# Attention run as one sequence of rounds in a fixed TensorE order, with the softmax factors moved behind the products and some small transfers moved to GpSimd's queue

## Chip, cores and metric

The kernel runs on one core of one Trainium2 chip. The metric is the device time of one execution in microseconds, and the median of three runs is compared. A core has five engines that each work through their own list of instructions in order: TensorE (PE; its weight loads are the separate rows PEld), VectorE (DVE), ScalarE (ACT), GpSimd (POOL) and SyncE (SP, which here only issues transfers).

## The reference

One decoder layer over 1024 positions of width 1024, in float32. One projection feeds three groups of heads, whose outputs are joined, projected and added to the input; a gated feed-forward part follows.

```
h = rms_norm(x, norm_mix);  proj = h @ w_in
y_conv = conv_mixer(p_conv)          # 256 channels, causal convolution of width 31
y_nsa  = nsa_mixer(p_nsa)            # 8 query heads, 2 KV heads, head size 64
y_rwkv = rwkv7_mixer(p_rwkv)         # 4 heads x 64, a recurrence over positions
x = x + concat(y_conv, y_nsa, y_rwkv) @ w_out
h = rms_norm(x, norm_ffn);  x = x + (silu(conv3(h @ w_gate)) * (h @ w_up)) @ w_down
return rms_norm(x, norm_final)

# nsa_mixer, for each block of 128 queries:
return gate0 * o_cmp + gate1 * o_sel + gate2 * o_win
# o_cmp: attention over 63 compressed blocks; o_sel: over the selected blocks, which with
# 16 blocks of 64 keys and top 16 are all keys up to the query; o_win: over the last 512 keys
```

Each of the three is a softmax of its own: exp(scores - max), divided by its sum, times the values.

## The kernel before

The work runs in stages. Input projection, convolution and the first half of RWKV fill the span up to some 400 us. Stage "2" is attention together with the second half of RWKV. Stage "o" is the output projection; then come the two feed-forward products.

Attention goes over eight tiles of 128 queries in the order 7, 6, 5, 4, 0, 3, 2, 1 (`attn_tile`, one call for each). A tile i has two branches: the window branch (br 2, min(i+1, 5) key tiles of 128) and the selected branch (br 1, i+1 key tiles). A branch has four units (r), each for one query head of both KV heads (g). For a unit TensorE forms the scores in PSUM banks "mm" (L893 with the high part of the keys, L894 with the low part), VectorE adds the mask and finds the extreme (L897), ScalarE takes the exponential and sums it (L904), VectorE forms gate over sum (L905, L906) and scales the 128 x W probabilities with it (L911), TensorE transposes them, two key tiles at a time, into a "tr" bank (L918), ScalarE copies that bank to SBUF (L921, tile "pT"), and TensorE multiplies with the values into the tile's one bank "av" (L926), which collects both branches and the compressed one (L862 to L865). At its end the bank is copied (L932, tile "mix") and stored to `md` in DRAM. In all there are 264 pairs of unit and key tile: 528 transposes and 528 products, which the trace counts as 1056 records.

The instructions of one engine stand in an order that a scheduler picked when the kernel was built; nothing by hand holds TensorE's order in attention. RWKV's steps are emitted with high priority and fall in among the attention.

RWKV works in four units: 00 and 01 before attention, 10 and 11 during it. A unit starts (S) with products on TensorE (L493) that give GA, whose blocks go through DRAM (`dn`, L503, and L506 back into sN). A forward substitution of 31 steps follows on GpSimd (L528 and L530, each step needing the one before). Its result goes through DRAM again (`dt` L534, `dtt` L535, then DF L543 and sN L546, L547), and TensorE takes it up at L550 (step V). Then the chain of states runs (step C, L591 to L611), and its end (L631, L636) gives the gated output, stored to `md` (L638). The 19 transfers of a unit are issued by SP.

GpSimd also forms the sums of the feed-forward weights during attention (`down_sums`, L945 to L948: 44 operations of 128 x 512, their loads at L943), between the steps of unit 10's substitution, and small parts of the compressed branch (L849, L857).

Stage "o" (`out_tile`) loads the joined outputs of 128 positions from `md` (L984, tile "mix"; the first half of it holds convolution and RWKV, the second attention), splits them in two parts (L120, L121) and multiplies with w_out (L229, "woh", "wol"), in 48 products for one tile of positions. The parts of w_out are loaded at L964 and L967.

## Time and profile before

| | us |
|---|---|
| median of 3 runs (lowest, highest) | 1515.36 (1514.93, 1518.39) |
| the profiled execution | 1516.71 |
| its span | 1515.0 |
| TensorE busy in the span | 1418.2 |
| VectorE, ScalarE, GpSimd busy | 1001.0, 684.0, 500.2 |
| attention, from the first scores to the last product (start) | about 402 to 731 |

The span is what the trace covers; 1.71 us of the profiled execution lie outside it. Busy time is the sum over an engine's instructions. A granted clock of 1.00 is TensorE's full speed in that stretch.

### The profile page before, as it was taken

The page shows a single profiled execution, that of the slowest core. Times are in us where ns is not written, and L with a number is a line of the kernel's source. Part 1 is how long each engine was busy: PE and PEld are TensorE (multiplying, and loading weights), DVE is VectorE, ACT ScalarE, POOL GpSimd, SP SyncE. Part 2 cuts the span into 40 slices and gives each one's busy share as a digit, 9 for nine tenths or more (in the row PEclk, how much of TensorE's full clock was granted, in tenths as well). Part 3 has the DMA queues.
Part 4 walks back from the last instruction along what each step waited for, and adds up shares of the span by engine and source line. Part 5 has one row for each costly group of instructions (what it writes and reads, how often), then busy time and mean ns, then how long its engine had stood idle before and what let it go on. Part 6 is the DMA issues. An engine that isn't in the chain of part 4 may idle for free.

```text
span 1515.0 us, 22973 instructions
## 1 busy us (share of the span) xinstructions
PE 1418.2 (94%) x8025; PEld 1128.7 (75%) x8025; DVE 1001.0 (66%) x2171; ACT 684.0 (45%) x1361; POOL 500.2 (33%) x607
## 2 busy tenths in 40 slices
PE   6999688999798999999599899999999999999997
PEld 5887566777666777767478677888888788888886
DVE  5346696454488587777446776775876876666675
ACT  5432255534155665776333353333333443445463
POOL 1003887910487204100000133453453443113310
PEclk9999887999699999999899999999999999999999
DMA  6133223434888301310742113332332333986633
GB/s 184 36 105 80 46 77 95 146 89 119 246 259 270 101 21 41 81 43 16 226 121 84 57 56 98 105 112 84 104 119 91 104 104 111 383 295 213 207 91 111
DMA packets 206680, 186.71 MB, mean 123 GB/s; under 512 B 56355, under 2 KB 145764, under 8 KB 206564
## 3 DMA queue, kind: packets, MB, share of 16 engines
q1 hardware_dynamic: 206564, 185.24, 39.5%
q8 instruction: 63, 1.03, 0.3%
q14 instruction: 53, 0.43, 0.1%
HBM read 126.99 MB, written 58.20 MB: 122 GB/s over the span
## 4 chain that ended last, share of the span: by engine, by line
PE 78%; DVE 10%; DMA 4%; POOL 2%; issue 2%; ACT 2%; SPq 1%; DVEq 0%; ACTq 0%; POOLq 0%
PE mm L229 13%; PE gb L229 12%; PE rw L229 10%; PE ga L229 8%; PE gc L229 8%; PE tr L229 5%; PE tr L918 4%; PE av L926 4%; PE mm L893 2%; PE mm L894 2%; POOL sx L528 1%; PE rw L493 1%; POOL sT L530 1%; DVE pp L897 1%; DVE pp L911 1%
## 5 line engine op out<-in xcount | busy, mean ns | idle before, releaser
L229 PE MATMUL mm<-hT,whi 128*128 128x512 f32 x608 | 201.6, 413 | 0.0
L229 PE MATMUL mm<-hT,wlo 128*128 128x512 f32 x304 | 126.1, 416 | 18.8 <-DVE wlo L121 18.8
L229 PEld LDWEIGHTS mm<-hT,whi 128*128 128x128 f32 x608 | 118.3, 197 | 28.5 <-issue 1.4
L921 ACT ACTIVATE pT<-tr 128x512 f32<-128x512 f32 (+1 forms) x152 | 79.8, 536 | 62.1 <-PE tr L918 59.0
L926 PE MATMUL av<-pT,V 128*64 128x128 f32 x1056 | 96.4, 289 | 1.3 <-ACT pT L921 1.1
L279 POOL TENSOR_TENSOR cacc<-cacc,ctap 128x512 f32<-128x512 f32 x60 | 91.6, 1550 | 15.0 <-ACT ctap L278 14.9
L229 PE MATMUL rw<-woh,mix 128*128 128x512 f32 x240 | 79.4, 406 | 17.0 <-ACT mix L120 17.0
L918 PE MATMUL tr<-idn,pp 128*128 128x128 f32 x528 | 91.6, 292 | 0.5 <-DVE pp L911 0.3
L121 DVE TENSOR_TENSOR sp<-rb,sp 128x512 fp32r<-128x512 f32 x66 | 57.1, 865 | 50.4 <-ACT sp L120 50.3
L1072 POOL TENSOR_TENSOR S<-wraw,wr 128x512 f32<-128x512 f32 x22 | 28.5, 1295 | 181.0 <-DVE or L107 79.2
L229 PEld LDWEIGHTS mm<-hT,wlo 128*128 128x128 f32 x304 | 59.9, 197 | 37.0 <-DVE wlo L121 20.1
L893 PE MATMUL mm<-KH,QS 128*128 128x512 f32 (+2 forms) x192 | 77.3, 407 | 10.0 <-DVE mx L897 7.7
L229 PE MATMUL rw<-sp,sp 128*128 128x512 f32 x330 | 86.1, 389 | 0.0
L229 PE MATMUL tr<-sp,sp 128*128 128x512 f32 x330 | 85.9, 389 | 0.0
L926 PEld LDWEIGHTS av<-pT,V 128*64 128x64 f32 x1056 | 59.9, 138 | 27.3 <-issue 13.0
L528 POOL TENSOR_TENSOR sx<-sN,sT 128x60 f32<-128x60 f32 (+24 forms) x124 | 47.4, 382 | 97.4 <-DMA sN<-dn 90.5
L918 PEld LDWEIGHTS tr<-idn,pp 128*128 128x128 f32 x528 | 56.5, 142 | 30.0 <-issue 27.9
L120 ACT ACTIVATE sp<-rb 128x512 fp32r<-128x512 f32 x66 | 41.6, 630 | 74.0 <-PE tr L229 37.5
L121 DVE TENSOR_TENSOR sp<-b,sp 128x512 fp32r<-128x512 f32 x88 | 68.8, 789 | 5.3 <-ACT sp L120 5.1
L229 PEld LDWEIGHTS rw<-sp,sp 128*128 128x128 f32 x330 | 62.0, 188 | 12.8
L229 PEld LDWEIGHTS tr<-sp,sp 128*128 128x128 f32 x330 | 62.0, 188 | 12.8
L904 ACT ACTIVATE pp<-pp,nm 128x640 f32<-128x640 f32 (+3 forms) x64 | 57.6, 904 | 23.7 <-DVE nm L902 22.1
(457 smaller groups left out, 3721.0 us busy)
## 6 DMA issues: line engine op xcount, KB each, us to landing
wraw<-in_ffn_w_up_dram SPq DMA_DIRECT2D x44, 256.0 KB
wr<-in_ffn_w_gate_dram SPq DMA_DIRECT2D x44, 256.0 KB
pdS<-prod SPq DMA_DIRECT2D x44, 256.0 KB
b<-pdS SPq DMA_DIRECT2D x44, 256.0 KB
rb<-tdT SPq DMA_DIRECT2D x44, 256.0 KB
pdA<-prod SPq DMA_DIRECT2D x33, 256.0 KB
b<-pdA SPq DMA_DIRECT2D x33, 256.0 KB
wraw<-in_w_in_dram SPq DMA_DIRECT2D x30, 256.0 KB
```

What stands on the lines that cost most here:

```text
L120: self.nc.scalar.activation(hi, src, AF.Copy)
L121: getattr(self.nc, eng).tensor_tensor(lo, src, hi.bitcast(F32), op=ALU.subtract)
L229: mm = lambda l, r, **k: self.nc.tensor.matmul(out, l, r, skip_group_check=more, **k)
L279: nc.gpsimd.tensor_tensor(t[:, o:o + 512], t[:, o:o + 512], z, op=ALU.add)
L528: v_.tensor_tensor(x, N[:, q, q + 1:32].unsqueeze(2).to_broadcast([P, n, w]), Tm[:, q, 0:w].unsqueeze(1).to_broadcast([P, n, w]), op=ALU.mult)
L893: pe.matmul(pts[g][:, 0:n], QS[:, r, g, :], KH[g][hf][:, ks], start=True, stop=False)
L894: pe.matmul(pts[g][:, 0:n], QS[:, r, g, :], KL[g][hf][:, ks], start=False, stop=True)
L904: s.activation(Ps[g], Ps[g], AF.Exp, bias=nm[:, g:g + 1], scale=-1.0, accum_out=sm[:, g:g + 1])
L918: pe.transpose(pt[:, o:o + P], Ps[g][:, kt * P:kt * P + P], self.idn)
L921: s.activation(pT[:, 0:n], pt[:, 0:n], AF.Copy)
L926: pe.matmul(av[g * 64:g * 64 + 64, r * P:r * P + P], self.V[kk // 2][:, kk % 2, vo + g * 64:vo + g * 64 + 64], pT[:, o:o + P], start=first ...
L1072: gp.tensor_tensor(t, x, y, op=op)
```

## The change

Attention becomes one function over all tiles. It lists the units, cuts each branch into rounds, and emits round after round: the transposes of round k, then the products of round k-1, then scores for the rounds ahead, as far as the six "pp" buffers go. A round has two items; an item is two pairs of unit and key tile (which may belong to different units, so that every "tr" bank is filled with four transposes), or the four transposes of the compressed branch or of the factors. Each TensorE instruction of attention is tied behind the one emitted before it (`pe`), so their order is held; instructions of RWKV and of stage "o" may still fall in between.

The probabilities are no longer scaled. Each branch collects its products in a bank of its own turn; gate over sum is formed once for a tile and branch ([128, 8], L905 and L906 before), spread by GpSimd to a [128, 512] tile "fx", transposed by TensorE, copied by ScalarE ("fs"), multiplied with the finished bank by VectorE and added to "mix" by GpSimd. The compressed branch has a bank of its own and starts "mix".

The 19 transfers of each RWKV unit (dn, sN, dt, dtt, DF, sN) are issued by GpSimd instead of SP. In the table of numbers pT goes from 5 to 9 buffers, pk from 1280 to 1024, and a new dvc=4 gives each fourth copy of a "tr" bank to VectorE. `down_sums` is emitted at the end of each tile, as before.

```diff
-                        nc.sync.dma_start(dn[p0:p0 + 8].rearrange("p s t -> s p t"), Gm[64 + blk * 32:96 + blk * 32, :, blk * 32:blk * 32 + 32])
+                        nc.gpsimd.dma_start(dn[p0:p0 + 8].rearrange("p s t -> s p t"), Gm[64 + blk * 32:96 + blk * 32, :, blk * 32:blk * 32 + 32])
         N = self.sN.rearrange("p (a b) -> p a b", b=32)
         for g in range(4):
-            nc.sync.dma_start(N[g * 32:g * 32 + 32], dn)
+            nc.gpsimd.dma_start(N[g * 32:g * 32 + 32], dn)
...
-            nc.sync.dma_start(u.dt[:, :, g, :], Tm[g * 32:g * 32 + 16])
-            nc.sync.dma_start(u.dtt[:, :, g, :], sTT[g * 32:g * 32 + 32])
+            nc.gpsimd.dma_start(u.dt[:, :, g, :], Tm[g * 32:g * 32 + 16])
+            nc.gpsimd.dma_start(u.dtt[:, :, g, :], sTT[g * 32:g * 32 + 32])
...
-        nc.sync.dma_start(DF[64:96], u.dt.rearrange("p s g c -> s p (g c)"))
+        nc.gpsimd.dma_start(DF[64:96], u.dt.rearrange("p s g c -> s p (g c)"))
         nc.gpsimd.memset(TT[96:128, :, 0:32], 0.0)
         dtt = u.dtt.rearrange("p c g t -> (c g) p t")
-        nc.sync.dma_start(TT[64:96, :, 0:32], dtt[:, 0:16])
-        nc.sync.dma_start(TT[96:128, :, 32:64], dtt[:, 16:32])
+        nc.gpsimd.dma_start(TT[64:96, :, 0:32], dtt[:, 0:16])
+        nc.gpsimd.dma_start(TT[96:128, :, 32:64], dtt[:, 16:32])
...
-                v.reciprocal(sm, sm)
-                v.tensor_tensor(sm, sm, gt[:, r:8:4, br], op=ALU.mult)
-                for g in range(2):
-                    if g < self.B["sc"]:
-                        s.activation(Ps[g], Ps[g], AF.Copy, scale=sm[:, g:g + 1])
-                    else:
-                        v.tensor_scalar(Ps[g], Ps[g], sm[:, g:g + 1], None, op0=ALU.mult)
...
+    def pe(self, *a, transpose=False, **k):
+        ins = (self.nc.tensor.transpose if transpose else self.nc.tensor.matmul)(*a, **k)
+        if self.pe_last is not None:
+            self.tc.add_manual_dep(ins.ins, self.pe_last.name, mybir.DependencyInfo(mybir.DependencyClass.NoSync, mybir.DependencyReason.DATA),
+                                   reason="attention")
+        self.pe_last = ins.ins
+        return ins
...
+    def attn_T(self, x, units):
+        pt = self.bank("tr")
+        y = [(units[n], kt, g) for n, kt in x for g in range(2)]
+        for n, (u, kt, g) in enumerate(y):
+            self.pe(pt[:, n * P:n * P + P], u.Ps[g][:, kt * P:kt * P + P], self.idn, transpose=True)
+        pT = self.xt([P, 512], "pT")
+        self.ncopy += 1
+        if self.B["dvc"] and self.ncopy % self.B["dvc"] == 0:
+            self.nc.vector.tensor_copy(pT, pt)
+        else:
+            self.nc.scalar.activation(pT, pt, AF.Copy)
+        return [(*z, pT[:, n * P:n * P + P]) for n, z in enumerate(y)]
+    def attn_factors(self, t, br):
+        nc = self.nc
+        F = t.sums[br]
+        nc.vector.reciprocal(F, F)
+        f2 = F.rearrange("p (r g) -> p g r", g=2)
+        nc.vector.tensor_tensor(f2, f2, t.gt[:, :, br].rearrange("p (g r) -> p g r", g=2), op=ALU.mult)
+        X = self.xt([P, 512], "pT", name="fx")
+        nc.gpsimd.tensor_copy(X.rearrange("p (a b) -> p a b", b=64), F.unsqueeze(2).to_broadcast([P, 8, 64]))
+        t.X[br] = X
+    def attn_AV(self, done):
+        for u, kt, g, pT in done:
+            t, r = u.t, u.r
+            if r == 0 and kt == 0 and g == 0:
+                t.av = self.bank("av")
+                t.first = [True, True]
+            vo = 128 if u.br == 2 else 0
+            kk = u.lo_k // P + kt
+            self.pe(t.av[g * 64:g * 64 + 64, r * P:r * P + P], self.V[kk // 2][:, kk % 2, vo + g * 64:vo + g * 64 + 64], pT,
+                    start=t.first[g], stop=r == 3 and kt == u.w - 1)
+            t.first[g] = False
...
+        for i in order:
+            for br in (2, 1):
+                items, half = [], []
+                if units:
+                    items.append(("f", len(units) - 1))
+                w = min(i + 1, 5) if br == 2 else i + 1
+                for r in range(4):
+                    u = type("Unit", (), {})()
+                    u.i, u.br, u.r, u.w = i, br, r, w
+                    for kt in range(w):
+                        half.append((len(units), kt))
+                        if len(half) == 2:
+                            items.append(("k", half))
+                            half = []
+                    units.append(u)
+                    if br == 2 and r == 1:
+                        items.append(("c", len(units) - 1))
+                rounds += [items[k:k + 2] for k in range(0, len(items), 2)]
+        rounds.append([("f", len(units) - 1)])
...
+        def cmp_av(t):
+            cav = self.bank("mm")
+            self.pe(cav, self.vcmp[0:t.n2], t.ct[0:t.n2], start=True, stop=True)
+            t.mix = self.xt([P, 512], "pT", name="mix")
+            s.activation(t.mix, cav, AF.Copy)
+        def fac_T(t, br):
+            pt = self.bank("tr")
+            for r in range(4):
+                self.pe(pt[:, r * P:r * P + P], t.X[br][:, r * P:r * P + P], self.idn, transpose=True)
+            t.fs = self.xt([P, 512], "pT", name="fs")
+            s.activation(t.fs, pt, AF.Copy)
+        def end(t, br):
+            v.tensor_tensor(t.fs, t.av, t.fs, op=ALU.mult)
+            nc.gpsimd.tensor_tensor(t.mix, t.mix, t.fs, op=ALU.add)
+            if br == 1:
+                self.st.dma_start(self.md[:, 4:8, t.i * P:t.i * P + P], t.mix.rearrange("p (r q) -> p r q", q=P))
+                done_tile()
+        issue(top[1])
+        late = []
+        for k, items in enumerate(rounds):
+            done, fs, cs = [], [], []
+            for z, x in items:
+                if z == "k":
+                    done += self.attn_T(x, units)
+                elif z == "c":
+                    cmp_T(units[x].t)
+                    cs.append(units[x].t)
+                else:
+                    fac_T(units[x].t, units[x].br)
+                    fs.append(units[x])
+            while gone[0] < len(units) and (units[gone[0]], units[gone[0]].w - 1) in [(u, kt) for u, kt, _, _ in done]:
+                gone[0] += 1
+            self.attn_AV(late)
+            late = done
+            for u in fs:
+                end(u.t, u.br)
+            far = top[min(k + 2, len(rounds) - 1)]
+            near = top[min(k + 1, len(rounds) - 1)]
+            issue(near)
+            while opened[0] <= far and used() + (1 if 2 * units[opened[0]].w * P <= self.B["pk"] else 2) <= self.B["pp"]:
+                issue(opened[0])
+            for t in cs:
+                cmp_av(t)
...
-        for n, i in enumerate(order):
-            self.attn_tile(i)
-            for f in self.B["ds"][n]:
+        ds = iter(self.B["ds"])
+        def done_tile():
+            for f in next(ds):
                 self.down_sums(f)
+        self.attention(order, done_tile)
```

What this does to the order of instructions is shown at three places. First TensorE at the point where RWKV's unit 10 is taken up again (L550, the products with DF); av are the products with the values, mm the scores, tr the transposes. Before:

```order
L918 MATMUL tr_5500<-idn,pp_5453 128x128
L893 MATMUL mm_5724<-KH_4511,QS_5699 128x384
L894 MATMUL mm_5724<-KL_4517,QS_5699 128x384
L926 MATMUL av_5138<-pT_5494,V_4535 64x128
L550 MATMUL rw_3768<-DF,GA_3505 32x32 x8
```

Of the change:

```order
L866 MATMUL av_5206<-pT_5362,V_4507 64x128 x2
L866 MATMUL mm_5399<-KH_4523,QS_5047 128x512
L866 MATMUL mm_5399<-KL_4529,QS_5047 128x512
L866 MATMUL mm_5400<-KH_4526,QS_5047 128x512
L866 MATMUL mm_5400<-KL_4532,QS_5047 128x512
L866 MATMUL mm_5407<-KH_4495,QS_5047 128x384
L866 MATMUL mm_5407<-KL_4501,QS_5047 128x384
L550 MATMUL rw_3768<-DF,GA_3505 32x32 x8
```

Before, 163 of the 528 products with the values (and two of the compressed branch) stand ahead of this L550, and it comes when tile 5's scores have begun; in the change 144 stand ahead of it, and it comes inside tile 6's selected branch.

Second, GpSimd at the end of unit 10's substitution, in the change (fx, fs and mix are the tiles named above; before, there are no transfers in this queue):

```order
L528 TENSOR_TENSOR sx<-sN,sT 128x8
L544 MEMSET sN 32x16x32
L530 TENSOR_TENSOR sT<-sT,sx 128x8
L534 DMA dt_3485<-sT 512x1x8 x4
L535 DMA dtt_3486<-sTT 256x1x32 x4
L941 COPY fx_5281<-sums_5069 128x512
L543 DMA DF<-dt_3485 32x16x32
L523 COPY sT<-sI 128x256
L546 DMA sN<-dtt_3486 32x16x32
L547 DMA sN<-dtt_3486 32x16x32
```

Between the first and the last step of this substitution stood 44 operations of down_sums and four of the compressed branch; now 41 of down_sums, four of the compressed branch, two copies to fx and two additions to mix stand there.

Third, TensorE at the end of attention. Before (rw<-woh,mix is the first output tile of stage "o", tr<-idn,pp are transposes of probabilities):

```order
L918 MATMUL tr_7958<-idn,pp_7943 128x128 x4
L926 MATMUL av_7725<-pT_7935,V_4537 64x128 x4
L926 MATMUL av_7725<-pT_7963,V_4537 64x128 x4
L631 MATMUL rw_4437<-idn,gyc_4414 128x128 x4
L636 MATMUL rw_4445<-lora_772,lw_w 128x512
L229 MATMUL rw_8134<-woh_7974,mix_8120 128x512
L229 MATMUL rw_8134<-wol_7975,mix_8120 128x512
```

In the change, where the first output tile begins, among the products of tile 3 and the scores of tile 2:

```order
L866 MATMUL av_7196<-pT_7244,V_4535 64x128 x4
L866 MATMUL av_7196<-pT_7251,V_4537 64x128 x4
L866 MATMUL mm_7315<-KH_4511,QS_7263 128x384
L866 MATMUL mm_7315<-KL_4517,QS_7263 128x384
L229 MATMUL rw_8014<-woh_7854,mix_8000 128x512
L229 MATMUL rw_8014<-wol_7855,mix_8000 128x512
L229 MATMUL rw_8042<-woh_7860,mix_8000 128x512
L229 MATMUL rw_8042<-wol_7861,mix_8000 128x512
L866 MATMUL mm_7316<-KH_4514,QS_7263 128x384
```

RWKV's last rows (L631, L636) now stand 31 rows ahead of the first row of stage "o", the 48 products of the first output tile lie among the attention of tiles 3, 2 and 1, and the first product of the second output tile stands directly behind the last product of attention. On SP the loads of w_out stand ahead of the end of attention.

## Rows read from the trace of the kernel before

**Rows 1.** The page: busy time of each engine, its share of the span

```profile
PE 1418.2 (94%) x8025; PEld 1128.7 (75%) x8025; DVE 1001.0 (66%) x2171; ACT 684.0 (45%) x1361; POOL 500.2 (33%) x607
```

**Rows 2.** Busy us by stretch: PE, PEld, DVE, ACT, POOL, clock, DMA share, GB/s

```profile
400.00:450.00 50.00, 43.70 (x287) 32.59 (x288) 37.75 (x110) 22.62 (x46) 39.13 (x53) 0.87 0.86 265
450.00:500.00 50.00, 45.39 (x370) 33.06 (x369) 41.38 (x121) 27.42 (x55) 39.06 (x54) 0.93 0.80 258
...
600.00:650.00 50.00, 48.42 (x394) 34.77 (x394) 40.88 (x185) 33.40 (x94) 9.95 (x32) 1.00 0.25 62
700.00:735.00 35.00, 32.80 (x298) 23.02 (x297) 25.73 (x106) 24.40 (x63) 1.30 (x2) 1.00 0.16 46
735.00:760.00 25.00, 11.87 (x42) 9.31 (x43) 6.39 (x10) 4.41 (x7) 0.56 (x1) 0.73 1.02 320
```

**Rows 3.** Timeline of PE at the end of attention: start, us, instruction [idle before]

```profile
729.95 0.66 PE L918 MATMUL tr<-idn,pp 128*128 128x128 f32 x4
730.53 0.66 PE L926 MATMUL av<-pT,V 128*64 128x128 f32 x8
731.35 0.66 PE L926 MATMUL av<-pT,V 128*64 128x128 f32 x8 [0.16 <-ACT pT L921]
...
732.52 1.12 PE L636 MATMUL rw<-lora,lw_w 64*128 64x512 f32 x2
746.97 0.80 PE L229 MATMUL rw<-woh,mix 128*128 128x512 f32 x1 [13.32 <-ACT mix L120]
...
748.41 0.63 PE L229 MATMUL rw<-wol,mix 128*128 128x512 f32 x1
...
754.37 0.39 PE L229 MATMUL rw<-woh,mix 128*128 128x512 f32 x1
755.93 0.50 PE L229 MATMUL rw<-woh,mix 128*128 128x512 f32 x1 [1.16 <-ACT mix L120]
```

**Rows 4.** Timeline of SP's issues in the same stretch

```profile
736.02 0.43 SPq L638 DMA_DIRECT2D md<-gz  x1
...
741.14 0.43 SPq L984 DMA_DIRECT2D mix<-md  x1
```

**Rows 5.** Groups by line, 400 to 735 us: count | busy us, mean ns | idle before

```profile
L921 ACT ACTIVATE pT<-tr 128x512 f32<-128x512 f32 (+1 forms) x152 | 79.8, 536 | 62.1 <-PE tr L918 59.0 <-issue 1.8
...
L911 DVE TENSOR_SCALAR pp<-pp,sm 128x640 f32<-128x640 f32 (+7 forms) x128 | 66.6, 562 | 1.3
...
L906 DVE TENSOR_TENSOR sm<-sm,gates 128x2 f32<-128x2 f32 x64 | 13.8, 216 | 1.2
...
L905 DVE RECIPROCAL sm<-sm 128x2 f32<-128x2 f32 x64 | 10.2, 160 | 17.1 <-ACT pp L904 16.8
...
L947 POOL TENSOR_TENSOR wlo<-wlo,wraw 128x512 f32<-128x512 f32 x4 | 5.4, 1340 | 0.0
```

**Rows 6.** Timeline of POOL: first and last step of unit 10's substitution

```profile
404.67 0.24 POOL L528 TENSOR_TENSOR sx<-sN,sT 128x31 f32<-128x31 f32 x1 [16.36 <-DMA sN<-dn]
...
503.11 0.46 POOL L530 TENSOR_TENSOR sT<-sT,sx 128x8 f32<-128x8 f32 x1
```

**Rows 7.** Busy us by stretch, columns as in rows 2: that substitution

```profile
404.60:503.60 99.00, 88.81 (x668) 64.47 (x670) 81.16 (x234) 51.75 (x104) 81.46 (x111) 0.91 0.82 261
```

**Rows 8.** Timeline of SP's issues behind that substitution

```profile
503.76 0.59 SPq L534 DMA_DIRECT2D dt<-sT  x1
```

**Rows 9.** L550 on PE from 513 to 520 us: duration, first and last start

```profile
L550 PE MATMUL rw<-DF,GA x32: 190/192/212, 514.9 to 515.9; 32*32 32x32 f32 x32
```

**Rows 10.** Products with the values (L926) alone, by stretch: PE, PEld busy (records)

```profile
402.00:514.90 112.90, 30.98 (x326) 19.47 (x326) 0.92 0.77 241
514.90:600.00 85.10, 24.40 (x291) 15.17 (x290) 1.00 0.14 36
600.00:732.00 132.00, 40.96 (x440) 25.28 (x440) 1.00 0.18 48
```

**Rows 11.** Waits between 150 and 200 us: us in total, times, longest

```profile
PE mm L229 <- DVE wlo L121: 15.6, 2, 11.6
```

156 lines of the change are left out of this document (85 added, 71 removed).

## Prediction

> **What bounds the kernel now.** I read the busy times first. TensorE works 94% of the span and no other engine over 66% [rows 1], so time is won only where TensorE waits, runs at a lower clock, or does less. The change gives it no less to do, so I looked for its waits around attention in the table of stretches [rows 2]. Three places stand out. From 400 to 500 us TensorE lacks 6.3 + 4.6 = 10.9 us, at a clock of 0.87 and 0.93, while GpSimd is busy for 78 of 100 us and the transfers for over 80%. The tail of attention lacks little: 1.6 us in 600 to 650 and 2.2 us in 700 to 735. Then comes a hole: from 735 to 760 TensorE works 11.9 of 25 us.
>
> The products with the values tell the pace, four records for a unit's key tile: 326 records are 81.5 key tiles in 112.9 us, 1.39 us each; then 1.17 us, and 1.20 us from 600 us on [rows 10]. RWKV's work is in all three. So attention is slow only in its first stretch, by about 0.22 us for each of 81 key tiles, 18 us, of which 10.9 us is open idling.
>
> The timeline of the hole [rows 3]: the last product starts at 731.35, RWKV's last row at 732.52 lasts 1.12, and the first product of the output projection comes at 746.97 after 13.32 us of idling, put down to ScalarE's split of mix. SP's issues say why [rows 4]: RWKV's last result is stored at 736.02, and the load of mix that needs it goes out at 741.14. So RWKV's late end, not attention's, is the cause. After the idling a product takes 0.63 us instead of 0.39 (748.41 against 754.37), and 1.16 us is lost once more at 755.93.
>
> **The change part by part.**
>
> *The hole.* The order now has RWKV's end 31 rows ahead of the first output product, that output tile inside attention, and the second tile behind the last product. What can go is 13.3 us of idling, about 12 products at 0.24 us too much (2.9 us), and 1.2 us: 17 us. What stays: the first output product still needs RWKV's result stored, loaded and split. Before, that took 746.97 - 733.64 = 13.3 us, some of it a crowded queue (320 GB/s, [rows 2]); 31 rows of short products cover about 6 us; the w_out loads come earlier now. I keep 2 us, bounds 0 and 7. The next output tiles have 48 products each ahead, at 0.2 us or more some 10 us, which cover the last tile's chain of factors. **Gain 15 us (10 to 17).**
>
> *The factors.* VectorE loses 66.6 + 13.8 + 10.2 = 90.6 us [rows 5]. It gains 33 copies (at ScalarE's 0.54, 17.8 us), 16 small pairs (0.16 + 0.22, 6 us) and 16 products of 128 x 512 (at L911's 0.56, 9 us): net 58 us less. ScalarE has 152 copies before and 99 + 16 + 8 now, 29 less by 0.54: 16 us less. TensorE gets 64 transposes more; four cost 0.58 us with the turn to products [rows 3], 16 times: 9 us at most. But banks of four full transposes save turns: 132 banks where there were 152, 20 turns less. I put these at nothing, bounds -9 and +6. Neither VectorE nor ScalarE was the bound where TensorE is full, so their relief buys only what TensorE waits for: the idling of the first stretch and the 3.8 us of the tail. With the gaps between score and copy filled by a fixed look-ahead of two rounds, **gain 6 us in the tail (0 to 15)**.
>
> *The first stretch.* It has the same relief, but a new tie: each branch now ends on GpSimd (a copy to fx, an addition to mix), and RWKV's transfers stand in that queue too. GpSimd's stretch from 404.67 to 503.6 [rows 6] has 81.5 us of work in 99 [rows 7]: the substitution's 62 steps and 44 operations of down_sums of about 1.3 us [rows 5]. The order of the change puts 41 of these, two copies and two additions into it: -4 and +4 us. So the substitution again takes 99 us, and TensorE can't take up L550 before it. Before, the way from 503.6 over eight transfers of 0.6 us issue [rows 8], DF and sN to L550 at 514.9 [rows 9] was 11.3 us. No transfer of GpSimd is in this trace; its issue costs between nothing (the engine only writes the command, and four dn no longer stand behind SP's key loads, which could start the stretch up to 5 us earlier) and twice SP's 0.6 us (11 us more over 19). I take 2 us more: L550 at 517, bounds 510 and 526.
>
> TensorE arrives earlier. Ahead of L550 stand 19 products less, 9.5 key tiles; at 0.6 us without scores (two key tiles in 1.2 us, [rows 3]) to 1.17 us with all, that is 6 to 11 us, I take 8. At the old pace it comes at 507, with the idling recovered at 496. It then waits 10 to 20 us. The idling recovered is worth nothing, and against the same work before (507) L550 at 517 is a **loss of 10 us (0 to 19)**. The factors of tile 7's second branch stand 26 steps and some seven sums ahead of that end, about 25 us, so at 490, close to when TensorE wants them; that wait would be part of the same one. Behind L550 GpSimd has no sums left to do. Unit 11's own L550 comes after 160 products more instead of some 220, so its substitution has less cover; GpSimd is free then, and I put it at nothing, at worst 5 us.
>
> *SP.* It no longer stands in line for the substitution. In unit 00 TensorE waits 15.6 us, 11.6 at once, on VectorE's split of a weight [rows 11], which stood behind a copy that waits for GpSimd's last step. The order puts one such split ahead of the copy, the next still behind: **gain 4 us (0 to 8)**. GpSimd pays there with eight issues in a queue that also adds the convolution's taps; TensorE's rows for unit 00 stand 74 rows later, which covers it.
>
> *A rule against it.* VectorE is busy 81 of 99 us during this substitution [rows 7], and this trace has no transfer issued by GpSimd, so no row shows what the two do to each other. The Trainium skill ("SBUF — State Buffer", section "SBUF: two separate sides") states that GpSimd writes the descriptors of its own transfers, can't while VectorE runs some copies and scalings from SBUF to SBUF, and that transfers issued by SP are immune. It gives 620 ns against 3100 ns for one such case, so an estimate by that page is 2.5 us for each of 11 transfers behind the substitution, 27 us instead of the 2 above, which would make the sum below 1526. The scalings of L911 that the change removes are of that kind. No run here shows any of it.
>
> **The sum.** Against the profiled execution's 1516.7 us (span 1515.0 and 1.7 outside it, 1.3 above the median): -15 (hole) - 6 (tail) + 10 (L550) - 4 (unit 00) = -15, so **1501.5 us**.
>
> **The rivals.**
>
> *A. GpSimd is not late (0.25).* The stretch starts early, its idling of 17.5 us [rows 7] shrinks because SP brings the weights sooner. Then L550 costs nothing and most of the 10.9 us comes back too: -15 - 8 - 10 - 4, with 8 from the tail: 1480, from 1473 to 1490. Against it: the stretch was already 82% work, and each load waits for a buffer that the sums free.
>
> *B. The transfers are slow on GpSimd, slower than before (0.17).* Place: the 19 transfers around each substitution; the engine stands still while it issues, and VectorE's work (81 of 99 us, [rows 7]) may hold it. Price: each 0.1 us on a transfer is 1.9 us at L550. At 1.6 us a transfer instead of 0.6, that is 19 us, less the 2 already counted, and some 6 of it again in unit 00 or 11: 1525, from 1520 to 1540. It decides from 0.8 us extra for each transfer on.
>
> *C. The held order itself waits (0.13).* TensorE must follow the rounds even when an exponential is late; before, the scheduler had other rows there. For it: ScalarE's copies already waited 59 of 62 us on transposes [rows 5], so the loop is tight. A wait of 0.06 us on each of 264 key tiles is 16 us: 1517, between 1511 and 1520, no change.
>
> **How the numbers follow.** The forecast (0.45) lies between 1490 and 1511, by the bounds of L550 and the tail. A measurement of this kernel tells about 0.3%, 4.5 us, from no change. Faster by more is the forecast and A: 0.70. Within it: C, 0.13. Slower: B, 0.17. Eight in ten reach from the middle of A to the lower part of B: 1478 to 1523.
>
> **What would show it.** Right: TensorE waits for DF at L550 around 510 to 526, 8 to 20 us, with GpSimd's substitution until then; no idling over 4 us between the last product of attention and the output projection; the clock at 1.00 there. For A: L550 before 505 without a wait. For B: GpSimd's queue waits in the transfer lines and more than 14 us from its last step to L550. For C: many short waits of transposes on ScalarE's exponential. The prediction is wrong if the hole reappears inside attention as a wait of the first output product, or if the rate behind L550 leaves 1.1 to 1.2 us for a key tile.

## The result and the profile after

The changed kernel takes 1565.98 us (1563.34 to 1568.35, four runs) against 1516.88 us (1514.93 to 1523.27, four runs) of the kernel before: a ratio of 1.032 with a 95% interval of 1.0294 to 1.0346, so 49 us slower. The prediction said 1501.5 us, with eight chances in ten for 1478 to 1523.

The page of the changed kernel, its first line and the busy times (columns as in [rows 1]):

```profile
span 1563.9 us, 22966 instructions
PE 1446.2 (92%) x8089; PEld 1163.2 (74%) x8089; DVE 956.0 (61%) x1996; ACT 669.6 (43%) x1324; POOL 561.7 (36%) x715
```

VectorE and ScalarE do less, 45 and 14 us (58 and 16 were forecast); neither was the bound. TensorE is busy 28 us longer and idles 118 us instead of 97. To see where, I set three marks in each trace: the first compressed scores, the end of the last product with the values, and the first feed-forward product. Before they lie at 400, 732 and 823 us, after at 418.7, 804 and 871.6. So the stages up to attention lose 19 us, attention loses 53, and the output projection gains 24. The stretches of the changed kernel (columns as in [rows 2]):

```profile
400.00:450.00 50.00, 39.82 (x223) 32.45 (x224) 22.81 (x62) 10.53 (x22) 30.14 (x45) 0.66 0.91 256
450.00:500.00 50.00, 41.60 (x315) 30.10 (x316) 29.28 (x85) 21.43 (x39) 36.99 (x47) 0.93 0.77 243
...
54.00:418.70 364.70, 331.20 (x1691) 262.28 (x1691) 188.30 (x330) 131.78 (x240) 174.94 (x250) 0.87 0.34 97
418.70:804.00 385.30, 345.37 (x2923) 269.70 (x2922) 218.62 (x733) 203.19 (x457) 154.87 (x254) 0.94 0.36 106
356.30:381.30 25.00, 23.12 (x200) 18.95 (x199) 9.02 (x30) 8.76 (x17) 0.00 (x0) 0.59 0.18 53
...
804.00:871.60 67.60, 60.23 (x266) 49.40 (x265) 32.38 (x86) 16.40 (x43) 1.26 (x1) 0.92 0.40 140
```

and the same stretches of the kernel before:

```profile
54.00:400.00 346.00, 315.55 (x1699) 248.63 (x1697) 195.91 (x332) 132.51 (x241) 157.37 (x208) 0.91 0.36 100
327.50:352.50 25.00, 25.00 (x230) 20.43 (x230) 7.75 (x24) 10.67 (x22) 0.10 (x1) 0.93 0.29 86
400.00:732.00 332.00, 318.19 (x2805) 236.78 (x2806) 249.31 (x891) 207.87 (x478) 109.17 (x187) 0.97 0.37 111
...
732.00:823.30 91.30, 74.34 (x319) 59.56 (x319) 42.45 (x101) 25.90 (x58) 2.57 (x2) 0.91 0.51 159
```

*Up to the first scores* TensorE idles 33.5 us where it idled 30.5. The loss is in the clock: 0.87 of 364.7 us leaves 47.4 us not granted, 0.91 of 346 us leaves 31.1. These 16.3 us and the 3 us of idling are the whole shift, as closely as a clock of two decimals tells. One place carries half of it: in the 25 us from RWKV's unit 01 taken up again (L550) the granted clock is 0.59, before 0.93. TensorE is busy 23.1 of these 25 us, so what fell is the clock, not the work.

*In attention* TensorE idles 39.9 us (385.3 less 345.4), before 13.8, and is busy 27.2 us longer. Of these, the output tile that moved in takes 10.8 (48 products at 0.23) and the 64 transposes of factors 9.3 (four in 0.58); the rest, some 7 us, lies beside a clock of 0.94 instead of 0.97. *Behind it*, the 23.7 us gained are these same 10.8 and 12.9 more.

TensorE's timeline in the changed kernel (columns as in [rows 3]):

```profile
356.34 1.19 PE L550 MATMUL rw<-DF,GA 32*32 32x32 f32 x32
...
360.18 1.65 PE L563 MATMUL rw<-sN,VA 64*64 64x64 f32 x26 [0.77 <-issue]
...
507.57 0.66 PE L866 MATMUL av<-pT,V 128*64 128x128 f32 x8
516.62 1.77 PE L866 MATMUL tr<-idn,pp 128*128 128x128 f32 x7 [8.39 <-ACT fs L1030]
...
541.46 1.19 PE L550 MATMUL rw<-DF,GA 32*32 32x32 f32 x32
...
746.59 0.40 PE L229 MATMUL rw<-woh,mix 128*128 128x512 f32 x1
...
803.37 0.66 PE L866 MATMUL av<-pT,V 128*64 128x128 f32 x8
811.40 0.80 PE L229 MATMUL rw<-woh,mix 128*128 128x512 f32 x1 [7.37 <-DVE xn L1124]
```

Unit 10 is taken up at 541.46, without a wait. The longest wait of attention is the one of 8.39 us: seven transposes of probabilities, whose exponentials are done by 506.9, wait for a "tr" bank until "fs", the copy of a branch's factors, has emptied one. ScalarE's timeline and GpSimd's, both of the changed kernel, show who is late:

```profile
506.66 0.19 ACT L916 ACTIVATION_READ_ACCUMULATOR pp<-pp,nm 128x1 f32 x1
515.51 0.58 ACT L851 ACTIVATE cmp<-cmp 128x448 f32<-128x448 f32 x1 [8.66 <-POOL cmp L850]
515.99 0.58 ACT L1030 ACTIVATE fs<-tr 128x512 f32<-128x512 f32 x1
```

```profile
428.88 0.24 POOL L528 TENSOR_TENSOR sx<-sN,sT 128x31 f32<-128x31 f32 x1 [0.25 <-DMA sN<-dn]
...
506.10 1.29 POOL L1076 TENSOR_TENSOR whi<-wlo,whi 128x512 f32<-128x512 f32 x1 [3.54 <-DMA wlo<-in_ffn_w_down_dram]
...
513.06 1.26 POOL L1076 TENSOR_TENSOR wlo<-wraw,wlo 128x512 f32<-128x512 f32 x1 [1.22 <-DMA wraw<-in_ffn_w_down_dram]
514.28 0.31 POOL L530 TENSOR_TENSOR sT<-sT,sx 128x60 f32<-128x60 f32 x1
514.54 0.94 POOL L850 TENSOR_TENSOR cmp<-cmp,cmx 128x448 f32<-128x448 f32 x1
...
527.41 0.20 POOL L530 TENSOR_TENSOR sT<-sT,sx 128x8 f32<-128x8 f32 x1
527.91 2.54 POOL L534 DMA_DIRECT2D dt<-sT  x4 [0.30 <-POOL sT L530]
...
533.51 0.67 POOL L543 DMA_DIRECT2D DF<-dt  x1
```

ScalarE has finished an exponential at 506.9 and could copy the factors. But its queue has the compressed exponential (L851) first. That waits for GpSimd's L850, which stands behind steps of the substitution and down_sums, and two of these sums, at 506.10 and 513.06, wait 3.54 and 1.22 us for a weight from DRAM. None of these links feeds the transposes that stood still.

### The profile page after: what moved, and what is told of

It is laid out like the page before. It is cut to its first block, busy times and chain, and to the rows that moved or that the text cites. A ratio compares the mean times of both kernels' runs of the same rounds, so it can differ in the third digit from the quotient of the medians.

```text
span 1563.9 us, 22966 instructions
## 1 busy us (share of the span) xinstructions
PE 1446.2 (92%) x8089; PEld 1163.2 (74%) x8089; DVE 956.0 (61%) x1996; ACT 669.6 (43%) x1324; POOL 561.7 (36%) x715
## 4 chain that ended last, share of the span: by engine, by line
PE 73%; DVE 8%; DMA 7%; POOL 3%; issue 3%; ACT 3%; SPq 1%; DVEq 0%; ACTq 0%; POOLq 0%
PE mm L229 13%; PE gb L229 11%; PE rw L229 11%; PE ga L229 8%; PE gc L229 8%; PE tr L229 5%; PE mm L866 4%; PE tr L866 3%; PE av L866 3%; POOL sT L530 1%; PE pm L493 1%; DMA tdT<-whi 1%; POOL sx L528 1%; ACT pp L916 1%; DMA x<-in_x_dram 1%
## 5 line engine op out<-in xcount | busy, mean ns | idle before, releaser
L866 PE MATMUL tr<-idn,pp 128*128 128x128 f32 x528 | 84.9, 293 | 30.9 <-ACT pp L916 12.7
L866 PEld LDWEIGHTS tr<-idn,pp 128*128 128x128 f32 x528 | 64.2, 148 | 48.3 <-ACT pp L916 15.8
L279 POOL TENSOR_TENSOR cacc<-cacc,ctap 128x512 f32<-128x512 f32 x60 | 87.6, 1474 | 23.5 <-ACT ctap L278 23.3
L930 ACT ACTIVATE pT<-tr 128x512 f32<-128x512 f32 x99 | 57.0, 592 | 64.9 <-PE tr L866 63.9
L866 PE MATMUL av<-pT,V 128*64 128x128 f32 x1056 | 82.1, 292 | 0.0
L908 DVE CUSTOM_DVE_ANT_0 pp<-mm,msel 128x512 f32<-128x512 f32 (+3 forms) x96 | 49.9, 554 | 35.3 <-PE mm L866 35.0
L229 PEld LDWEIGHTS tr<-sp,sp 128*128 128x128 f32 x330 | 61.9, 188 | 12.9
```

The source lines that it names most:

```text
L229: mm = lambda l, r, **k: self.nc.tensor.matmul(out, l, r, skip_group_check=more, **k)
L279: nc.gpsimd.tensor_tensor(t[:, o:o + 512], t[:, o:o + 512], z, op=ALU.add)
L866: ins = (self.nc.tensor.transpose if transpose else self.nc.tensor.matmul)(*a, **k)
L908: v.tensor_tensor_reduce(Ps[g][:, ka - lo_k:kb - lo_k], pts[g][:, o:o + kb - ka], mask(ka, kb), 1.0, 3.4e38, ALU.add, ALU.min, mx[:, g, c: ...
L930: self.nc.scalar.activation(pT, pt, AF.Copy)
```

## The experiments

The theories. **Order**: moving transfers to another engine changes the order that the scheduler gives TensorE ahead of attention, and that order costs clock. **Held**: TensorE, held to the rounds, stands still where the scheduler had put other rows. Their rivals: **queue**, the transfers themselves are slow on GpSimd; **links**, the copy to fx and the addition to mix come late in GpSimd's queue; **arithmetic**, the 64 transposes, the banks and the rest of the new form cost. In the expectations on record, theory 1 is the loss ahead of attention (*order* or *queue*; 1a to 1d are its forms), theory 2 is *links*, and theory 3 is *held* (3a to 3e say through what). Ratios are against the kernel before, with 95% intervals; its median in the same runs lay between 1515.3 and 1517.8 us.

**Transfers back on SP**, the rest of the change kept.

```diff
-            nc.gpsimd.dma_start(N[g * 32:g * 32 + 32], dn)
+            nc.sync.dma_start(N[g * 32:g * 32 + 32], dn)
...
```

> The change with RWKV's 19 transfers per unit issued by SP again; attention as changed. Its TensorE order ahead of attention is that of before. Theory 1 (the transfers cost the time ahead of attention: TensorE takes unit 00 and 01 up later, closed up, at half clock): first compressed scores at 400 to 404 us instead of 418.7, and the time 1566 - 16 to 20 = 1546 to 1550. Theory 2 (GpSimd's queue in attention, with RWKV's transfers in it, is what holds TensorE): first scores unchanged near 418, the gain of 10 to 25 us comes behind them. Theory 3 (the held order of attention is the loss): 1560 or more, no large change.

1560.18 us (1559.18 to 1561.41), 1.0285 [1.0253, 1.0318]. First scores at 404.2 us, 14.5 earlier than in the change, as theory 1 had them; but attention takes 396.7 us instead of 385.3, and the time is the one of theory 3. The stretch of attention:

```profile
404.20:800.90 396.70, 351.70 (x2922) 274.48 (x2922) 223.26 (x733) 203.75 (x457) 133.48 (x220) 0.92 0.35 106
```

**Transfers on GpSimd alone**, in the kernel before.

```diff
-            nc.sync.dma_start(N[g * 32:g * 32 + 32], dn)
+            nc.gpsimd.dma_start(N[g * 32:g * 32 + 32], dn)
...
```

> The kernel before with only RWKV's transfers issued by GpSimd; its attention stays. Theory 1: first compressed scores near 417 us instead of 400, time 1516 + 16 to 20 = 1532 to 1536. Theory 2: the loss is at unit 10 (L550 later than 525 instead of 514.9), 1520 to 1530. Theory 3: within 5 us of before.

1536.16 us (1532.47 to 1542.09), 1.013 [1.0088, 1.0173]: 21 us slower. Three stretches of this kernel, the two of the marks and the one behind unit 10's substitution:

```profile
54.00:419.00 365.00, 331.16 (x1691) 262.20 (x1691) 188.54 (x330) 132.07 (x241) 175.51 (x251) 0.87 0.34 98
419.00:751.50 332.50, 320.63 (x2805) 237.12 (x2804) 253.09 (x892) 208.16 (x478) 130.24 (x221) 0.97 0.36 106
...
523.00:536.00 13.00, 12.80 (x118) 9.54 (x118) 7.30 (x26) 8.07 (x17) 6.00 (x10) 1.00 0.48 91
```

The first is that of the changed kernel almost to the row, at a clock of 0.87; attention is as long as before. So the loss ahead of attention, 19 us of the 21, belongs to the transfers and to nothing in attention, as theory 1 had it. GpSimd's timeline at unit 10, and two scalings of VectorE in the same time:

```profile
521.41 2.93 POOL L534 DMA_DIRECT2D dt<-sT  x4 [0.30 <-POOL sT L530]
524.34 2.31 POOL L535 DMA_DIRECT2D dtt<-sTT  x4
526.53 0.77 POOL L543 DMA_DIRECT2D DF<-dt  x1
...
522.74 1.36 DVE L911 TENSOR_SCALAR pp<-pp,sm 128x896 f32<-128x896 f32 x2
```

That is 0.58 to 0.77 us each, where SP took 0.59 [rows 8], while VectorE is busy 7.3 of 13 us. The Trainium skill ("SBUF — State Buffer", section "SBUF: two separate sides") gives 620 ns for a transfer of GpSimd alone and 3100 ns beside a copy of VectorE, and the prediction's estimate from it was 2.5 us more for each. This estimate is not borne out: the four dt, beside the two scalings, took 0.62 us longer than the four dtt, all four together. At unit 00 DF does go out later, at 183.70 us against 177.78 before, but TensorE's row for it stands at 202.7, 19 us behind that, and doesn't wait. So *queue* falls as the cause of these 21 us.

**The change without the tie.**

```diff
-        if self.pe_last is not None:
+        if False:
```

> The change without the tie between TensorE's instructions of attention, so that their order is picked freely again; all else as changed. Theory 3: TensorE's idling behind 418 us falls from some 47 us to 15 to 20, and with it the half clock: 1530 to 1545. Theory 2: a chain through GpSimd (compressed branch, factors) still holds it: 1555 to 1575. Theory 1: the 418.7 us of the first scores stay, whatever comes behind.

1547.6 us (1542.89 to 1550.92), 1.02 [1.0162, 1.0237], 18 us less than the change. Attention idles 12.3 us, about as before the change, so theory 3 holds there. With 17.9 us of waiting for mix in front of the output projection the idling behind the first scores falls from 47 to some 30 us only, not to 15 to 20, and the time came out 3 us above theory 3's range. The stretch of attention:

```profile
420.20:761.80 341.60, 329.33 (x2869) 251.91 (x2868) 217.04 (x717) 196.81 (x442) 150.69 (x252) 0.97 0.35 104
```

The three runs now make a ladder: 21 us for the transfers, 11.4 for the new arithmetic with a free order (with the changed numbers of buffers in it), 18.4 for the tie.

**Copy to fx, addition to mix and the compressed branch on VectorE** instead of GpSimd.

```diff
-        nc.gpsimd.tensor_copy(X.rearrange("p (a b) -> p a b", b=64), F.unsqueeze(2).to_broadcast([P, 8, 64]))
+        nc.vector.tensor_copy(X.rearrange("p (a b) -> p a b", b=64), F.unsqueeze(2).to_broadcast([P, 8, 64]))
...
-            nc.gpsimd.tensor_tensor(t.mix, t.mix, t.fs, op=ALU.add)
+            v.tensor_tensor(t.mix, t.mix, t.fs, op=ALU.add)
```

> The change with all of attention's GpSimd work (the compressed branch's two operations, the copy to fx, the addition to mix) done by VectorE; RWKV's transfers stay on GpSimd. Theory 2: the wait of 8.4 us on fs at 516 us and the waits of a few us beside it go, and half clock behind them: 1541 to 1556. Theory 3: only these 8 us at most go, VectorE's 20 us more cost something: 1558 to 1572. Theory 1: first scores still near 418 us.

1583.48 us (1581.55 to 1584.45), 1.0435 [1.0395, 1.0474], 17 us more, above every range. *Links* gains nothing this way. VectorE now stands in a chain of the same kind, as its timeline shows:

```profile
514.25 0.39 DVE L532 COPY sTT<-sT 128x256 f32<-128x256 f32 x1 [15.37 <-POOL sT L530]
```

This copy waits for the last step of the substitution, 15.37 us, with attention's work for VectorE behind it, and TensorE waits 15.04 us, until 515.72, for the exponential that needs that work.

**Two halves of the transfers**, each in the kernel before: first only dn and sN ahead of the substitution (L503, L506), then only the others, behind it.

```diff
-            nc.sync.dma_start(N[g * 32:g * 32 + 32], dn)
+            nc.gpsimd.dma_start(N[g * 32:g * 32 + 32], dn)
```

> The kernel before with only the 8 transfers ahead of each substitution (dn, sN) on GpSimd. Theory 1a (it is the 11 behind the substitution: in GpSimd's queue the convolution's taps stand between them, and TensorE takes the units up later, closed up, at half clock): first compressed scores within 6 us of 400, time 1515 to 1523. Theory 1b (the cost lies ahead of the substitution, where GpSimd stands still for dn to land): first scores at 415 us or later, 1530 or more.

1505.09 us (1501.6 to 1510.74, ten runs), 0.9922 [0.9897, 0.9946].

> The kernel before with only the 11 transfers behind each substitution (dt, dtt, DF, sN) on GpSimd. Theory 1a: unit 00's L550 after 195 us instead of 179.7, first compressed scores at 412 to 419 us, 1528 to 1537. Theory 1b: within 6 us of before, 1515 to 1522.

1519.63 us (1515.92 to 1528.24, ten runs), 1.0027 [1.0005, 1.0049]. Minus 11 and plus 4 do not add up to plus 21, so the price is not one per transfer. Neither form of theory 1 had the first half faster than before; for the second half 1b had the time. The first scores come at 387.5 and at 395.8 us, both earlier than before. The second half loses its 4 us in attention, 352.8 us long instead of 332.0, of which 12 come back behind it. The stretch of the first half:

```profile
54.00:387.50 333.50, 304.00 (x1673) 239.30 (x1672) 191.36 (x328) 131.97 (x236) 170.35 (x228) 0.94 0.37 104
...
323.80:348.80 25.00, 25.00 (x240) 21.06 (x240) 10.84 (x34) 11.79 (x25) 0.10 (x1) 1.00 0.35 101
```

A clock of 0.94 leaves 20.0 us not granted, and 1.00 in the 25 us behind unit 01's L550, where 240 records stand instead of 200. Taking the clock's loss off the first scores gives 369 us before, 371 in the change, 371.5 with all transfers, 367.5 and 365 with the halves, 366 with the transfers back on SP. This is *order*: the work ahead of attention takes about the same time, less its clock. Over the whole span the granted clock is 0.962 before, 0.970 and 0.959 with the halves, 0.951 with all transfers, which leaves 57.6, 45.1, 62.3 and 75.4 us not granted: 12.5 less, 4.7 and 17.8 more than before, where these spans are 12.8 shorter, 4.6 and 22.8 longer.

In the traces 767 and 1507 of TensorE's rows (products and transposes) stand ahead of the first L550 row of units 00 and 01 before, 794 and 1531 with the first half, 801 and 1551 with the second, 841 and 1600 with both and in the change. Ahead of the first scores this list depends on the transfers alone, whatever attention is. In all nine kernels of this case with the transfers on SP its 1947 rows stand as before, all but four at the same place, and the first scores come at 395.9 to 404.3 us. In the four with all 19 on GpSimd and no tie ahead of attention the rows stand as in the change, again but for four at most, and the first scores come at 414.4 to 420.2; in the four with the first half, at 385.3 to 392.3. One list thus varies by 6 to 8 us from kernel to kernel, less than these lists differ. The list and the issuing engine change together in all of them, so that the list alone sets the clock is argued, not shown.

**The units tied back**: all transfers on GpSimd in the kernel before, and the second of the projection's product groups behind L550 of units 00 and 01 tied to that L550, so that 777 and 1435 rows stand ahead of the units: unit 00 nearly at its old place, unit 01 72 rows ahead of it. (By the traces the units stand 74 and 93 rows later with all transfers on GpSimd; the expectation has 115 for unit 01.)

```diff
+            self.mm3(pt[:n], [(hi[k], lo[k], hT[0][half][k], hT[1][half][k]) for k in range(8)], tie=self.solved if self.nsolve == 2 else None)
```

> The kernel before with all transfers on GpSimd (1536), with two ties on TensorE: the second half of the next projection stands behind the take-up of unit 00 and of unit 01, as it nearly does in the kernel before. Theory 1c (the transfers are as quick on GpSimd; what costs 21 us is that TensorE's order takes the units up 74 and 115 rows later): unit 00's L550 row starts at 186 to 192 us instead of 202.7, first compressed scores at 392 to 408 instead of 419, time 1512 to 1526. Theory 1d (the transfers themselves or GpSimd's queue cost it): first scores at 413 or later, 1530 to 1540.

1550.89 us (1549.33 to 1558.31), 1.0229 [1.0199, 1.0258]. The first scores come at 428.8 us, where theory 1d had them; the time is above both ranges. The clock behind unit 01's L550 came back, 0.90 over 25 us, but TensorE now waits for the unit (6.6 us for DF and 9.4 for cum, idling 47.1 us up to the first scores), and 48.7 us of clock are still not granted. So nearly at its old place unit 00 does wait for the transfers, and a *queue* in this form isn't ruled out. The tie mended the clock at one place and broke others; it settles that place, not the whole.

**Free order, and only dn and sN on GpSimd.**

> The change with its order free and only the 8 transfers ahead of a substitution on GpSimd, as in the run that took 1505. Free order cost 11 us more than the attention of before when all transfers were on GpSimd (1547.6 against 1536.2), 8 of which are the 64 transposes of factors. If that is the price of the new arithmetic wherever the transfers are: 1512 to 1520. If it came from the order ahead of attention: 1500 to 1508.

1516.8 us (1509.74 to 1530.0, ten runs), 0.9995 [0.9968, 1.0022]. Its edit takes out the tie and puts the 11 other transfers back on SP. Against the half alone, the new arithmetic costs 11.7 us, as it did (11.4) beside all transfers. The two don't lie in the same place, though. Beside all transfers attention itself is 9.1 us longer (341.6 against 332.5), the size of the 9.3 us of transposes. Beside the half it is only 3.8 longer (346.7 against 342.9), and TensorE waits 17.9 us for mix in front of the output projection, where it waited 8.2. So *arithmetic* is a term of its own, but the transposes are shown as its cause in the first pair alone.

**The held order, changed in size.** All with the transfers on SP. First rounds of one item, with the look-ahead, which counts rounds, raised from 1 and 2 to 3 and 5.

```diff
-                rounds += [items[k:k + 2] for k in range(0, len(items), 2)]
+                rounds += [[z] for z in items]
...
-            far = top[min(k + 2, len(rounds) - 1)]
-            near = top[min(k + 1, len(rounds) - 1)]
+            far = top[min(k + 5, len(rounds) - 1)]
+            near = top[min(k + 3, len(rounds) - 1)]
```

> The run with SP's transfers (1560.2) and rounds of one item instead of two, with the same reach of scores ahead in items; the order is still held. Theory 3a (a round's eight transposes take both tr banks at once, so the next round waits for ScalarE's two copies, which stand behind exponentials): the products with the values alternate with four transposes and the idling behind 404 us falls from 53 to under 30 us; 1530 to 1545. Theory 3b (any order held by hand waits here, since exponentials and factors come late): 1555 to 1565.

1583.27 us (1581.14 to 1589.04), 1.0448 [1.0413, 1.0484]: 23 us worse and above both ranges, the waits now on the products for the copies of a "tr" bank, 21.4 us in 17 waits. Then seven "pp" buffers (and eight pT) with scores up to four rounds ahead:

```diff
-                      QS=2, pp=6, q8=2, pT=9, dvc=4, ...
+                      QS=2, pp=7, q8=2, pT=8, dvc=4, ...
...
-            far = top[min(k + 2, len(rounds) - 1)]
+            far = top[min(k + 4, len(rounds) - 1)]
```

> The run with SP's transfers and held order (1560.2) with scores issued up to four rounds ahead instead of two and seven pp buffers instead of six (pT 8 for room). Theory 3d (the scores come too late in the held order, so transposes wait for exponentials): attention's idling falls from 53 to 35 us or less, 1535 to 1550. If the place of the scores isn't it: 1555 to 1565.

1543.86 us (1540.74 to 1547.3), 1.0177 [1.0128, 1.0227]: 16 us better, in theory 3d's range of time, with the waits for "pp" and for "fs" down to 1.5 us each; those for the copies to pT stay, and one of 10.5 us for mix stands in front of the output projection, so that TensorE still idles some 45 us behind the first scores. Last, every second copy of a "tr" bank on VectorE (dvc=2 for 4):

> The run with SP's transfers and held order (1560.2), with every second copy of a tr bank on VectorE instead of every fourth, so that a round's two copies run side by side. Theory 3c (the copies stand behind exponentials in ScalarE's queue, and the held order waits for them): idling behind 404 us falls from 53 to 35 us or less, 1535 to 1550. If VectorE's queue holds its copies as long: 1555 to 1570.

1557.67 us (1552.77 to 1564.97), 1.0275 [1.0234, 1.0315]: no difference, so theory 3c falls: a round's copies side by side don't help.

**Two links of the chains taken away.** The 44 operations of down_sums left out (the output lacks the sums of the feed-forward weights), and the stores of mix issued by GpSimd instead of SP; both with the transfers on SP.

```diff
-        tt(b[0, 0], b[0, 1], b[0, 0], op=ALU.subtract)
...
```

> The run with SP's transfers and held order (1560.2), without the 44 operations of down_sums on GpSimd; loads and stores stay, so the feed-forward weights' sums are left out of the computation. Theory 2 (GpSimd's queue is what the held order waits for): the wait of 6.8 us on fs near 501 us goes, unit 10 is taken up some 30 us or more earlier, and the time falls to 1530 to 1545. Theory 3 (the held order waits for ScalarE's and VectorE's own pieces): the idling behind the first scores stays above 40 of 53 us; 1550 to 1562.

1547.24 us (1546.0 to 1550.66), 1.0199 [1.0178, 1.0219]: 13 us less, between the two ranges. Attention is 10.8 us shorter (385.9 instead of 396.7), the waits for "fs" fall from 11.6 to 1.4 us, and unit 10 is taken up at 461.2 instead of 518.8. So the chain through GpSimd's sums is real, but it is a third of what the tie costs here (42 us, see below).

```diff
-                self.st.dma_start(self.md[:, 4:8, t.i * P:t.i * P + P], t.mix.rearrange("p (r q) -> p r q", q=P))
+                nc.gpsimd.dma_start(self.md[:, 4:8, t.i * P:t.i * P + P], t.mix.rearrange("p (r q) -> p r q", q=P))
```

> The run with SP's transfers (1560.2) and the store of attention's result to md issued by GpSimd, which forms it, instead of SP. If the 8 us of idling behind the last product of attention come from SP, which stands at the last tile's store with the loads of x behind it: they go, with the half clock behind them, 1548 to 1553. If the load of x comes late for another reason: 1558 to 1562.

1559.3 us (1555.86 to 1565.8), 1.0289 [1.0251, 1.0328], no difference. In the change SP waits from 785.9 to 806.7 with this store, and eight loads of x stand behind it, which is the wait of 7.37 us at 811.40. With the transfers on SP that wait is 8.1 us; with the store moved it is 1.5 us, and a new one of 4.3 us for mix follows.

**Which rows the tie hurts.** With the transfers on SP, once the scores are set free of the tie and once only the scores are tied, to each other.

```diff
-                self.pe(pts[g][:, 0:n], t.QS[:, r, g, :], KH[g][hf][:, ks], start=True, stop=False)
+                self.nc.tensor.matmul(pts[g][:, 0:n], t.QS[:, r, g, :], KH[g][hf][:, ks], start=True, stop=False)
...
```

> The run with SP's transfers and held order, with scores and the opening of a tile taken out of the tie; transposes and products are still held. Theory 3e (it is the tie of the scores to the rounds that makes TensorE wait): as with a wholly free order, idling 13 to 25 us instead of 53, time 1520 to 1535. If the tie between transposes and products is what waits: 1550 or more, idling over 40.

1518.12 us (1510.11 to 1524.43, ten runs), 1.0009 [0.9984, 1.0034]: 42 us less than with the tie, a little below theory 3e's range. The waits of TensorE from 395 to 805 us (us in total, times, longest), first with all rows tied, then with the scores free:

```profile
PE tr L866 <- ACT fs L1030: 11.6, 3, 6.8
PE tr L866 <- ACT pp L916: 9.2, 9, 2.0
PE tr L866 <- ACT pT L930: 8.0, 6, 2.6
PE tr L866 <- DVE pT L928: 4.2, 2, 4.1
```

```profile
PE mm L904 <- DVE mx L908: 5.1, 6, 2.2
...
PE tr L866 <- POOL cmp L858: 2.0, 1, 2.0
...
PE tr L866 <- ACT pT L930: 1.1, 2, 0.9
...
PE tr L866 <- ACT pp L916: 0.2, 1, 0.2
```

These 33 us of waits in front of transposes shrink to 1.3 us once the scheduler may put scores there, beside a new one of 2.0 us for the compressed branch. The stretch of attention:

```profile
399.00:751.00 352.00, 335.73 (x2874) 263.03 (x2874) 219.07 (x724) 199.20 (x448) 131.30 (x218) 0.92 0.38 112
```

It goes from 396.7 to 352 us. Of these 44.7 us, 28.7 are idling, 3.5 clock, and 10.8 the output tile, which this order leaves behind attention. There the last product and the output projection follow each other within 0.7 us.

> The counterpart: only scores, and the opening of a tile, are tied to each other; transposes, products and factors are free. Theory 3e would still have waits only where scores wait for banks: 1520 to 1545. If the tie between transposes and products is the loss: 1520 to 1535, idling under 25 us. Both runs near 1560 would mean that neither tie alone is the cause; both near 1528 that only the two together are.

1526.01 us (1515.1 to 1530.75, ten runs), 1.0043 [1.0012, 1.0074]. That is 8 us more than with the scores free. Either tie alone stays within 9 us of the kernel before; both together take 34 and 42 us more than one of them: what costs is tying the scores to the transposes and products. *Held* stands, and this is its part.

**The best of both.** Scores free, and only dn and sN on GpSimd; beside it the kernel before with that half of the transfers once more.

> The new attention with its scores free (1518 with SP's transfers) and the 8 transfers ahead of each substitution on GpSimd (1505 with the attention of before). If the gain ahead of attention adds up: first compressed scores near 387 us and 1503 to 1511. If not: 1513 to 1522.

1508.32 us (1501.4 to 1518.3, twelve runs), 0.9949 [0.9923, 0.9975]. The time adds up as forecast; the first scores come at 392.3 us, in an execution that is among its slowest (1516.86).

> The kernel before with only the 8 transfers ahead of each substitution on GpSimd, again: 1502 to 1508, that is 0.6 to 0.9% below before, if its gain holds in another run.

1509.2 us (1502.39 to 1514.17, twelve runs), 0.994 [0.9917, 0.9963]. The gain holds, a little smaller than in its first run (0.8%). Both are faster than the kernel before, by 0.5 and 0.6%, and can't be told from each other: the rewriting of attention, in the best form found here, adds nothing that could be measured to moving eight of a unit's 19 transfers.

## Why the prediction was wrong

**The hole: its size right, its sign missed.** 15 us (10 to 17) were forecast, 12.9 came. The wait of 13.3 us [rows 3] is gone; a wait of 7.37 us stands in its place, through SP's queue instead of RWKV's end, which the 2 us kept for it (0 to 7) just missed. The prediction's own sign, no idling over 4 us there and a clock of 1.00, failed with it: the clock is 0.92.

**The transfers' price: right, and without weight.** Substitution to L550 was forecast at 13.3 us and took 13.9 (527.6 to 541.46); the substitution itself at 99 us and took 98.7. L550 was forecast at 517 and came at 541.46: the substitution started 24.2 us later, at 428.88 instead of 404.67 [rows 6], and that is the difference. Rival B, the only one that had a slower kernel, fell with it. The wait of TensorE at L550, 8 to 20 us, didn't come, since TensorE itself was later than DF.

**Unit 00: the first failed step.** The prediction gave 4 us for SP's freedom and held that TensorE's rows of unit 00, "74 rows later, which covers it", cost nothing. The wait it named did shrink: VectorE's split of a weight cost 18.8 us from 100 to 260 us before and 9.4 after. But waits for ev (8.2) and cum (5.9) came instead. TensorE's waits in that stretch (columns as in [rows 11]), before:

```profile
PE mm L229 <- DVE wlo L121: 18.8, 3, 11.6
PE rw L591 <- DVE rH L601: 4.9, 1, 4.9
```

and after:

```profile
PE mm L229 <- DVE wlo L121: 9.4, 1, 9.4
PE mm L229 <- DVE ev L686: 8.2, 1, 8.2
PE pm L474 <- DVE cum L472: 5.9, 1, 5.9
```

The waits are nearly as long as they were, and the first scores came 18.7 us later, 16.3 of them in clock, half of that behind the take-up of unit 01. The prediction counted that shift as cover, and never asked what TensorE's rows beside the unit would be. With all transfers on GpSimd and nothing else that is 21 us.

**The tail: the second failed step.** The prediction put the relief of VectorE and ScalarE at a gain of 6 us, and the 64 transposes at nothing (bounds -9 and +6). In a free order the new arithmetic cost 11.4 and 11.7 us in the two pairs that measured it, 9.1 and 3.8 of them in attention. The relief bought nothing that showed, and the fixed look-ahead, which was to fill the gaps between score and copy, made them: with the scores free of it, 33 us of waits in front of transposes became 1.3. Attention behind L550 runs at 1.31 us a key tile (192 key tiles in 262.5 us less the output tile's 10.8), where before it took 217.1 us for 182.5, 1.19; a rate outside 1.1 to 1.2 was one of the prediction's signs of being wrong.

**Rival C had the mechanism and part of the price.** It gave the held order 16 us in many short waits and counted it against the forecast's gains. Together with the transfers on GpSimd the tie costs 18.4 us, so that size was near; with them on SP setting the scores free takes off 42. What it lacked was the form: not only many short waits on the exponential (12.7 us in 12) but single long ones (8.39), in which an engine's queue passes on a delay from a part of the program that has nothing to do with it.

The sum itself, 1516.7 - 15, gives 1501.7 and not 1501.5; nothing hangs on that.

**What stays open.** Why the scheduler answers two halves of the transfers with orders that gain 11 us and lose 4, and both with one that loses 21, the traces don't show; that gain and loss lie in TensorE's clock, they do. That its order alone sets this clock isn't shown: the attempt to put the order back by hand moved the loss instead of removing it. Why TensorE waits longer for mix behind attention in the free order beside the half of the transfers stays open too. The change with its tie off and all transfers on SP wasn't run, so the tie's price beside SP rests on the scores' part alone.

## What to carry to other kernels

A transfer that moves to another queue is also a change to the order in which every engine's work is laid out: compare the places of the affected products on the bound engine before costing the transfer. In an order held by hand a row that is ready waits behind one that is not; here it cost little to tie the scores among themselves, or the transposes and products, and much to tie both together, so leave the rows that need little (here the scores) free to fill. Look at what stands ahead of a link in its engine's queue, not at the engine's busy share: GpSimd was 36% busy and ScalarE 43%, and the wait of 8.39 us came through both.

## What the runs showed that was not expected

TensorE at a granted clock of 0.59 while it was busy 23.1 of 25 us: behind unit 01's L550 the small products of RWKV (32x32 and 64x64) stood closed up, and the engine had gaps of 0.24 and 0.77 us among them; with 512-column products between them the same 25 us had 0.93 before and 1.00 with half of the transfers moved. So 0.59 is mostly the lower of its two levels, 1.2 GHz. A stretch that looks full in the busy share can still be a dear one. GpSimd's transfers cost its queue 0.49 to 0.81 us each and landed, in the median of a kind, 1.9 to 3.3 us after the issue.
